# Fourth mixer: the state space part in chunks of 8 steps, with states at the chunk ends alone

## The chip, the cores and the metric

The kernel runs on one core of one Trainium2 chip, in one launch. The metric is the device time of that core in microseconds (us), the median of several runs. Its engines are TensorE (PE, matrix products; PEld its weight loads), VectorE (DVE), ScalarE (ACT), GpSimd (POOL, hardly used here) and SyncE (SP), which issues most of the DMAs. Each engine takes its instructions in the order in which they stand in its queue, so an instruction that waits also holds up all that stands behind it.

## The reference, cut to what matters

The model is a row of four mixer layers, the last two of them with a feed-forward part each, on a sequence of S = 512 rows of width 1024. The change touches the first half of the fourth mixer, the state space model (S5) on 256 channels in 16 groups of 16, with 64 complex states each:

```python
def s5_ssm(u, a_re, a_im, log_dt, b_re, b_im, c_re, c_im, d_skip, w_glu, b_glu):
    ...
    mag = jnp.exp(lr * dt)
    ab_re = mag * jnp.cos(li * dt)
    ab_im = mag * jnp.sin(li * dt)
    ...
    bu_re = jnp.einsum('bsgh,gph->bsgp', ug, bb_re)
    bu_im = jnp.einsum('bsgh,gph->bsgp', ug, bb_im)
    ...
    _, _, x_re, x_im = lax.associative_scan(combine, (aa_re, aa_im, bu_re, bu_im), axis=1)
    y = (jnp.einsum('bsgp,ghp->bsgh', x_re, c_re) - jnp.einsum('bsgp,ghp->bsgh', x_im, c_im)
         + d_skip[None, None] * ug)
    z = jax.nn.gelu(y)
    return z * jax.nn.sigmoid(z @ w_glu + b_glu)

def odd_mixer_2(t, ...):
    proj = t @ w_in
    y_c = s5_ssm(proj[..., :o1], ...)
    y_d = mla_attention(proj[..., o1:o2], proj[..., o2:o3], proj[..., o3:], ...)
    return jnp.concatenate([y_c, y_d], axis=-1) @ w_out
```

`mla_attention` has six heads; its keys and queries are made from two normed low rank pieces (`cn`, `cth` in the kernel). The state recurrence is x[t] = a x[t-1] + B u[t], and the output C x[t] + D u[t].

## The kernel before, in words

The program is a row of phases: two mixers (E1, O1), the third mixer E2 with its feed-forward part F0, the fourth mixer O2 with F1. Weights come by `wload` (line 126 is its DMA on SyncE): a raw piece `wr` (3 buffers), which ScalarE rounds to `wh` (line 133) and VectorE turns into the rest `wl` (line 116); five buffers of each. Every large product is three products of these halves (`mm3`, lines 145, 148, 149). An output projection `outp` keeps four pairs of PSUM banks, "P", "Z", "O" and "W" by their tags, one for each block of 128 rows.

Which instruction of an engine comes first is set by the Tile scheduler from priorities (`prio`), and `hold` ties one instruction behind another. `s5_setup` is called ahead of F0's output projection, so its vector work and its few products lie in F0; its products go to bank "W", which is also that of the fourth row block.

The state space part before: `s5_setup` writes for each of 8 channel blocks a table `rot` of 128 x 1280 (cosines and sines of all 512 steps and the block's input matrix) to DRAM. In O2 `s5(j)` fetches one (640 KB), makes two products of 128 x 512 (`bur`, `bui`), turns them with 12 vector operations of 128 x 512 and two scans, and `s5_out(j)` multiplies the result with C into a bank `py`. The 8 rounds are spread by `s5_step`: one ahead of `projS` (the projection of the low rank pieces), two ahead of the keys `kn` and queries `qn`, one behind each head, the rest behind the sixth. A head `attn` has four row blocks: scores `sc` in bank "Z", their largest `nm` (VectorE), exponentials `e` (ScalarE), reciprocal `rr` (VectorE), scaling (ScalarE, line 1177), transposes `pw` (line 203), copies `wt`; the product `po` of a head comes with the next head's `flush`. At the end come gelu, the gate's product (`pp<-zs`), its sigmoid, and `outp`.

## Time and profile before

| | us |
|---|---|
| three runs | 1712.09, 1715.67, 1715.69 (median 1715.67) |
| the profiled execution | 1711.21 |
| its span, first to last instruction | 1709.4 |
| TensorE busy | 1656.5 (97%) |
| VectorE busy | 950.2 (56%) |
| ScalarE busy | 677.7 (40%) |
| mean granted TensorE clock | 0.987 |

Busy time is a share of the whole span; the change is in two stretches of it, F0's output projection (from about 1001 us) and O2 (from about 1130 to 1340 us), and those are to be read by themselves. TensorE's busy time includes products whose ends are modelled, so it says where the engine had work, not that it ran at its best.

### The profile page before, as it was taken

To read this page: it belongs to the slowest core of one execution; us is meant where nothing else is said; L and a number is where in the kernel's file an instruction comes from. 1 tells how busy PE (TensorE), PEld (TensorE's weight loads), DVE (VectorE), ACT (ScalarE), POOL (GpSimd) and SP (SyncE) were. 2 spreads that over 40 slices of the span, in tenths; PEclk is the share of its full clock that TensorE was granted. 3 is DMA by queue.
4 is the path that set the end of the run, shared out by engine and by line. 5 is a ranking of instruction groups with operands and counts; after the bars stand their busy time and mean duration, and the time that the engine had idled before them with its cause. 6 is when DMAs were issued, how large, how long until landed. Compare 5 with 4: busy or idle time off the path is not lost.

```text
span 1709.4 us, 20684 instructions
## 1 busy us (share of the span) xinstructions
PE 1656.5 (97%) x8072; PEld 1323.6 (77%) x8072; DVE 950.2 (56%) x1801; ACT 677.7 (40%) x1192; POOL 2.0 (0%) x8
## 2 busy tenths in 40 slices
...
GB/s 203 85 38 74 91 181 105 75 25 99 62 205 116 74 87 33 84 187 99 99 99 97 91 151 200 165 123 81 31 31 197 111 100 99 99 95 90 99 160 50
DMA packets 53169, 179.07 MB, mean 105 GB/s; under 512 B 5696, under 2 KB 8256, under 8 KB 52944
## 3 DMA queue, kind: packets, MB, share of 16 engines
...
q14 instruction: 34, 0.28, 0.1%
q0 software_dynamic: 32, 0.07, 0.0%
HBM read 159.63 MB, written 18.10 MB: 104 GB/s over the span
## 4 chain that ended last, share of the span: by engine, by line
PE 85%; DVE 7%; ACT 4%; DMA 2%; issue 1%; ACTq 0%; DVEq 0%; SPq 0%
PE pp L145 17%; PE pp L148 17%; PE pp L149 17%; PE y L145 7%; PE y L149 7%; PE y L148 7%; PE pt L203 2%; PE po L368 2%; PE pl L625 1%; PE pw L203 1%; PE sc L822 1%; PE po L481 1%; DMA wr<-in_e2out 1%; PE pc L764 0%; DMA nw<-in_nw 0%
## 5 line engine op out<-in xcount | busy, mean ns | idle before, releaser
L116 DVE TENSOR_TENSOR wl<-wr,wh 128x1024 fp32r<-128x1024 f32 (+2 forms) x224 | 271.3, 1213 | 343.8 <-ACT wh L133 338.5
L133 ACT CAST wh<-wr 128x1024 fp32r<-128x1024 f32 (+2 forms) x224 | 233.4, 1043 | 523.4 <-PE pp L148 399.2
L148 PE MATMUL pp<-xl,wh 128*128 128x512 f32 (+1 forms) x1184 | 428.5, 362 | 0.0
L145 PE MATMUL pp<-xh,wh 128*128 128x512 f32 (+1 forms) x1184 | 426.0, 361 | 1.2 <-ACT xh L235 1.2
L149 PE MATMUL pp<-xh,wl 128*128 128x512 f32 (+1 forms) x1184 | 425.8, 360 | 0.0
L145 PEld LDWEIGHTS pp<-xh,wh 128*128 128x128 f32 x1184 | 223.8, 190 | 35.6 <-ACT xh L235 2.5
L148 PEld LDWEIGHTS pp<-xl,wh 128*128 128x128 f32 x1184 | 224.7, 190 | 33.8 <-issue 1.9
L149 PEld LDWEIGHTS pp<-xh,wl 128*128 128x128 f32 x1184 | 224.4, 190 | 33.4 <-issue 2.1
L145 PE MATMUL pp<-wh,xh 128*128 128x512 f32 (+1 forms) x320 | 126.4, 395 | 1.4 <-ACT sg L777 1.4
L148 PE MATMUL pp<-wl,xh 128*128 128x512 f32 (+1 forms) x320 | 126.5, 395 | 0.0
L149 PE MATMUL pp<-wh,xl 128*128 128x512 f32 (+1 forms) x320 | 125.4, 392 | 0.0
L145 PE MATMUL y<-wh,ah 128*128 128x512 f32 x288 | 112.7, 391 | 0.2
L148 PE MATMUL y<-wl,ah 128*128 128x512 f32 x288 | 112.3, 390 | 0.0
L149 PE MATMUL y<-wh,al 128*128 128x512 f32 x288 | 112.2, 389 | 0.0
L1238 DVE TENSOR_TENSOR act<-g,pp 128x512 f32<-128x512 f32 x44 | 30.2, 686 | 132.8 <-PE pp L149 131.4
L145 PEld LDWEIGHTS pp<-wh,xh 128*128 128x128 f32 x320 | 60.2, 188 | 13.4 <-ACT sg L777 1.8
L148 PEld LDWEIGHTS pp<-wl,xh 128*128 128x128 f32 x320 | 60.3, 188 | 11.7 <-issue 1.1
L149 PEld LDWEIGHTS pp<-wh,xl 128*128 128x128 f32 x320 | 60.2, 188 | 11.5 <-issue 0.6
L145 PEld LDWEIGHTS y<-wh,ah 128*128 128x128 f32 x288 | 54.1, 188 | 12.4 <-ACT bbz L998 1.1
L322 DVE TENSOR_TENSOR yn<-y,nw 128x512 f32<-128x512 f32 x48 | 31.8, 686 | 56.9 <-ACT yn L320 52.7
L790 DVE SCALAR_TENSOR_TENSOR ycv<-up,vec,ycv 128x512 f32<-128x512 f32 x90 | 63.2, 739 | 0.4
L149 PEld LDWEIGHTS y<-wh,al 128*128 128x128 f32 x288 | 54.1, 188 | 11.1
...
## 6 DMA issues: line engine op xcount, KB each, us to landing
...
```

What stands on the lines that cost most here:

```text
L116: return self.nc.vector.tensor_tensor(l, src, h.bitcast(F32), ALU.subtract)
L133: c = nc.scalar.copy(h, raw)
L145: r = mm(out, lhsT=a[0], rhs=b[0], start=first, stop=False)
L148: mm(out, lhsT=a[0], rhs=b[1], start=False, stop=False)
L149: return mm(out, lhsT=a[1], rhs=b[0], start=False, stop=last)
L203: self.nc.tensor.transpose(out, in_, self.ident)
L322: nc.vector.tensor_tensor(yn[j], yb[b][j], postw[j], ALU.mult)
L368: self.nc.tensor.matmul(po[:, tb * P : tb * P + P], lhsT=wt[:, sb, tb * P : tb * P + P], rhs=v[:, sb, c], start=sb == 0, stop=sb == tb)
L481: nc.tensor.matmul(po[r, sb * P :], lhsT=sv[:, sb, h * 64 : h * 64 + 64], rhs=wt[:, sb, sb * P :], start=sb == 0, stop=sb == 3)
L625: nc.tensor.matmul(pl[:, c4 * 64 : c4 * 64 + 64].rearrange("p (n x) -> p n x", x=H), lhsT=k[:, c4 * P : c4 * P + P], rhs=rh, start=True, s ...
L790: V.scalar_tensor_tensor(y, up[:, j : j + 512], self.v("dw", 4 * j + t), y, ALU.mult, ALU.add)
L1238: nc.vector.tensor_tensor(act[k // 4][:, k % 4], g, ps, ALU.mult)
```

## The change

The state space part now works in 64 chunks of 8 steps. Inside a chunk the output is one product with a triangular kernel (`s5k`), the chunk's input is brought to its end state by one product with a matrix `s5m`, and only the 64 end states are scanned, so that one set of vector operations and two scans over 512 columns (8 blocks x 64 chunks) serves all blocks.

- `s5_setup` makes those matrices: powers of a in small tables, 24 vector operations of 128 x 512 in four groups (`mi`, `mx`, `mg`), 16 transposes (`pbb`) and 32 products (`pk`) into bank "W", a small rotation table of 64 steps, and writes them to DRAM. The eight tables of 512 steps and the 16 products `pbb` are gone.
- `uT` is copied with its steps regrouped, written to DRAM (`s5u`) and read back by 16 DMAs of 16 x 8 x 64 elements (runs of 256 B).
- `s5_in`, behind the first piece of queries: 32 products of 64 x 64 into two banks "Z" (`z`), one set of vector operations, two scans.
- `s5_out`, behind heads 0 and 1: 24 products of 64 (or 63) columns in bank "P", a copy `yo`, 8 DMAs to DRAM (`s5y`, 256 B runs), one read back (`yt`), and on VectorE `yt` plus the skip term. Its matrices come by `s5_maps`, 2 + 8 DMAs.
- gelu may start behind head 4's exponentials, the sigmoid is tied behind the last.

```diff
 (s5_setup, the constants of the chunks)
+        for jj in range(2):
...
+            for ri, (p0, p1, op) in enumerate(((pr, pi, ALU.subtract), (pi, pr, ALU.add))):
+                m = self.U(name="mi")
+                m4 = m.rearrange("p (j s h) -> p j s h", j=4, s=8)
+                tt(m4, rh(bn[:, 0]), rp(p0, 0), ALU.mult)
+                tt(x4, rh(bn[:, 1]), rp(p1, 0), ALU.mult)
+                tt(m, m, x, op)
                 pt = self.bank("W", "pbb")
                 for c in range(4):
-                    self.nc.tensor.matmul(pt[32 * c : 32 * c + 32, 0:P], lhsT=w[2][:, 4 * jj + c], rhs=self.ident, start=True, stop=True)
...
+                    self.tr(pt[:, P * c : P * c + P], m[:, P * c : P * c + P])
+                o = self.U(name="mt")
+                nc.scalar.copy(o, pt)
+                nc.sync.dma_start(self.s5m[:, 1024 * ri + 512 * jj : 1024 * ri + 512 * jj + 512], o)
...
+            pk = self.bank("W", "pk")
+            for c in range(4):
+                for (lo_, hi_, rhs) in ((0, 16, lambda ri: cn[:, ri, 4 * jj + c]),
+                                        (16, 128, lambda ri: go[ri][:, c, 0:7].rearrange("p t h -> p (t h)"))):
+                    for ri in range(2):
+                        nc.tensor.matmul(pk[32 * c : 32 * c + 32, lo_:hi_], lhsT=bb[:, ri, 4 * jj + c], rhs=rhs(ri),
+                                         start=ri == 0, stop=ri == 1)
-        for j in range(8):
-            a, b, m = self.U(name="ra"), self.U(name="rb"), self.U(name="rm")
...
-            sincos(c, a, b, m)
-            nc.sync.dma_start(self.rot[j, :, 0:S], c)
-            nc.sync.dma_start(self.rot[j, :, S : 2 * S], a)
 (odd2)
         def keep(i, ps):
-            nc.scalar.copy(uT[:, i], ps)
+            nc.scalar.copy(uT[:, i].rearrange("p (s c) -> p c s", s=8), ps.rearrange("p (c s) -> p c s", s=8))
+            nc.sync.dma_start(ud[P * i : P * i + P], uT[:, i])
+            for s in range(8):
+                nc.sync.dma_start(ut[i][16 * s : 16 * s + 16].rearrange("p (g c) -> p g c", c=64), dv(ud)[:, s, 8 * i : 8 * i + 8])
+        def s5_in(after):
+            im, rt = self.A4(name="s5im"), self.A4(name="s5rt")
...
+            pz = [self.bank("Z", "z") for _ in range(2)]
...
+            for j in range(8):
+                for ri in range(2):
+                    for g in range(2):
+                        n = 2 * j + g
+                        r = nc.tensor.matmul(pz[ri][64 * g : 64 * g + 64, 64 * j : 64 * j + 64], lhsT=imv[:, ri, j, 64 * g : 64 * g + 64],
+                                             rhs=ut[n // 8][:, (n % 8) * 64 : (n % 8) * 64 + 64], start=True, stop=True)
...
+        def s5_out(jj, x, omv, tv):
+
+            py = self.bank("P", "py")
+            for n in range(8 * jj, 8 * jj + 8):
...
+                nc.tensor.matmul(py[:, o : o + 64], lhsT=tv[:, n % 8], rhs=ut[jj][:, o : o + 64], start=True, stop=False)
+                for ri in range(2):
+                    nc.tensor.matmul(py[:, o + 1 : o + 64], lhsT=omv[:, ri, j % 4], rhs=x[g][ri][:, j, 0:63], start=False, stop=ri == 1)
+            yo = self.U(name="yo")
+            nc.scalar.copy(yo, py)
+            for s in range(8):
+                nc.sync.dma_start(dv(yd)[:, s, 8 * jj : 8 * jj + 8], yo[16 * s : 16 * s + 16].rearrange("p (g c) -> p g c", c=64))
+            y = self.U(name="yt")
+            nc.sync.dma_start(y, yd[P * jj : P * jj + P])
+            V.scalar_tensor_tensor(y, uT[:, jj], self.v("dsk", jj), y, ALU.mult, ALU.add)
...
+                if pc == 0:
+                    xs = s5_in(kept)
...
         for hd in range(6):
             attn(hd)
-            s5_step(1, "P")
+            if hd < 2:
+                s5_out(hd, xs, *maps[hd])
+                maps[1] = s5_maps(1) if hd == 0 else None
...
-        s5_step(8, "P")
...
-            self.hold(r, self.last_e)
+            self.hold(r, gelu_after)
```


**The order, place 1: TensorE, F0's output projection.** `y` are its products (numbers 8143 to 8148 are the banks of the first three row blocks, 8149 and 8150 those of "W"; wh with ah are piece and activation). Before, the setup's products stood ahead of all `y`:

```order
L148 MATMUL pp1335_7803<-xl1084_5998,wh1333_7799 128x512
L149 MATMUL pp1335_7803<-xh1082_5996,wl1334_7800 128x512
L994 MATMUL pbb1341_7962<-cst_77,bb1340_7958 32x128 [waits DVE_49]
L994 MATMUL pbb1341_7962<-cst_77,bb1340_7958 32x128 x3
L994 MATMUL pbb1343_7974<-cst_77,bb1340_7958 32x128 x4
L145 MATMUL y1382_8143<-wh1391_8153,ah1393_8157 128x512 [waits Activation_49]
L148 MATMUL y1382_8143<-wl1392_8154,ah1393_8157 128x512
L149 MATMUL y1382_8143<-wh1391_8153,al1394_8158 128x512
L145 MATMUL y1383_8144<-wh1391_8153,ah1393_8157 128x512
L148 MATMUL y1383_8144<-wl1392_8154,ah1393_8157 128x512
```

Now there are 54 products `y` of the first three row blocks ahead of the first transpose, which waits for VectorE's `mi`:

```order
L149 MATMUL y1382_8148<-wh1394_8219,al1389_8158 128x512
L145 MATMUL y1377_8143<-wh1397_8251,ah1388_8157 128x512
L203 MATMUL pbb1352_8014<-cst_77,mi1351_8010 128x128 [waits DVE_49]
L203 MATMUL pbb1352_8014<-cst_77,mi1351_8010 128x128 x3
L148 MATMUL y1377_8143<-wl1398_8252,ah1388_8157 128x512
L149 MATMUL y1377_8143<-wh1397_8251,al1389_8158 128x512
L145 MATMUL y1378_8144<-wh1397_8251,ah1388_8157 128x512
...
L203 MATMUL pbb1355_8026<-cst_77,mi1354_8022 128x128 [waits DVE_49]
L203 MATMUL pbb1355_8026<-cst_77,mi1354_8022 128x128 x3
L1067 MATMUL pk1359_8044<-s5cn1349_8003,bb1346_7994 32x16 [waits Activation_49]
```

and the first `y` in a bank "W" comes only behind the second group of `pbb` and the first of `pk`, the second behind the last `pk`:

```order
L203 MATMUL pbb1366_8082<-cst_77,mi1365_8078 128x128 x3
L1067 MATMUL pk1370_8100<-s5cn1349_8003,bb1346_7994 32x16 [waits Activation_49]
L1067 MATMUL pk1370_8100<-s5cn1349_8003,bb1346_7994 32x16
L145 MATMUL y1383_8149<-wh1386_8153,ah1388_8157 128x512 [waits Activation_49]
L148 MATMUL y1383_8149<-wl1387_8154,ah1388_8157 128x512
...
L1067 MATMUL pk1370_8100<-mg1369_8095,bb1346_7994 32x112
L149 MATMUL y1383_8149<-wh1400_8283,al1403_8288 128x512
L145 MATMUL y1384_8150<-wh1386_8153,ah1388_8157 128x512 [waits Activation_49]
L148 MATMUL y1384_8150<-wl1387_8154,ah1388_8157 128x512
```

So the setup's products moved from ahead of the projection into it, and five weight pieces' worth of "W" products (8149, 8150) moved behind them.

**Place 2: O2, where the third piece of queries (the rotary part, `pp` of 128 x 384) is made.** Before, on TensorE, a projection, a score block `sc`, and the next projection follow each other:

```order
L145 MATMUL pp1644_9599<-wh1637_9576,cth1529_9146 128x384
L148 MATMUL pp1644_9599<-wl1638_9577,cth1529_9146 128x384
L149 MATMUL pp1644_9599<-wh1637_9576,ctl1530_9147 128x384
L1172 MATMUL sc1680_9722<-kn1608_9471,qn1610_9473 128x384 [waits DVE_49]
L145 MATMUL pp1649_9618<-wh1637_9576,cth1529_9146 128x384 [waits DVE_49,PE_49]
L148 MATMUL pp1649_9618<-wl1638_9577,cth1529_9146 128x384
L149 MATMUL pp1649_9618<-wh1637_9576,ctl1530_9147 128x384
L145 MATMUL pp1649_9618<-wh1637_9576,cth1529_9146 128x384
L148 MATMUL pp1649_9618<-wl1638_9577,cth1529_9146 128x384
L203 MATMUL pt1643_9594<-cst_77,r1640_9587 128x128 [waits DVE_49]
```

Now the last products `z` stand ahead of two score blocks, which wait for VectorE to leave the banks "Z", and of a projection that waits for the bank of the one before it:

```order
L1151 MATMUL z1605_9493<-uT1514_9032,s5im1602_9486 64x64 x2
L1151 MATMUL z1604_9492<-uT1514_9032,s5im1602_9486 64x64 x2
L1151 MATMUL z1605_9493<-uT1514_9032,s5im1602_9486 64x64 x2
L1274 MATMUL sc1662_9740<-kn1580_9413,qn1582_9415 128x384 [waits DVE_49,PE_49]
L1274 MATMUL sc1667_9756<-kn1580_9413,qn1582_9415 128x512 [waits DVE_49,PE_49]
L145 MATMUL pp1630_9625<-wh1618_9583,cth1523_9165 128x384 [waits DVE_49]
L148 MATMUL pp1630_9625<-wl1619_9584,cth1523_9165 128x384
L149 MATMUL pp1630_9625<-wh1618_9583,ctl1524_9166 128x384
L145 MATMUL pp1630_9625<-wh1618_9583,cth1523_9165 128x384
L148 MATMUL pp1630_9625<-wl1619_9584,cth1523_9165 128x384
L203 MATMUL pt1624_9601<-cst_77,r1621_9594 128x128 [waits DVE_49]
L203 MATMUL pt1624_9601<-cst_77,r1621_9594 128x128 x2
```

On VectorE the rows that free those banks stand within the vector operations of `s5_in` (`t11622_9595` and `t21623_9596` read the bank `pp1620_9587`):

```order
L1165 TENSOR_TENSOR sa1609_9533<-z1604_9492,s5rt1603_9487 128x512 [waits DMAHW3_49,PE_49]
L1166 TENSOR_TENSOR sb1610_9534<-z1605_9493,s5rt1603_9487 128x512 [waits DMAHW4_49,PE_49]
L1167 TENSOR_TENSOR sa1609_9533<-sa1609_9533,sb1610_9534 128x512 [waits DVE_49]
L1168 SCALAR_TENSOR_TENSOR yr1607_9531<-s5rt1603_9487,sa1609_9533 128x512 [waits DMAHW5_49,DVE_49]
L1166 TENSOR_TENSOR sb1610_9534<-z1604_9492,s5rt1603_9487 128x512
L1165 TENSOR_TENSOR sa1609_9533<-z1605_9493,s5rt1603_9487 128x512 [waits DVE_49]
L1167 TENSOR_TENSOR sa1609_9533<-sa1609_9533,sb1610_9534 128x512 [waits DVE_49]
L1168 SCALAR_TENSOR_TENSOR yi1608_9532<-s5rt1603_9487,sa1609_9533 128x512 [waits DVE_49]
L433 TENSOR_TENSOR t11622_9595<-pp1620_9587,cst_77 128x384
L1169 TENSOR_TENSOR sa1609_9533<-yr1607_9531,s5rt1603_9487 128x512 [waits DVE_49]
L1170 TENSOR_TENSOR sb1610_9534<-yi1608_9532,s5rt1603_9487 128x512
L434 TENSOR_TENSOR t21623_9596<-pp1620_9587,cst_77 128x6x32
```

So vector work that was spread over eight rounds now stands in one run, with the rotary operations between its rows.

**Place 3: behind head 0's output part.** Before, on VectorE, a row of the state space round stood between the heads' `nm` and `rr`, with a wait for VectorE alone:

```order
L1082 TENSOR_TENSOR yi1699_9776<-yi1699_9776,tab1695_9769 128x512
L1176 RECIPROCAL rr1713_9827<-nm1711_9823 128x1 [waits Activation_49]
L418 TENSOR_REDUCE nm1716_9839<-sc1715_9835 128x1
L1083 TENSOR_TENSOR yi1699_9776<-yr1698_9775,yi1699_9776 128x512 [waits DVE_49]
L416 MEMSET sc1720_9852 64x64 [waits PE_49]
L416 MEMSET sc1733_9894 64x64 [waits PE_49]
L1176 RECIPROCAL rr1718_9843<-nm1716_9839 128x1 [waits Activation_49]
L418 TENSOR_REDUCE nm1721_9856<-sc1720_9852 128x1 [waits DVE_49]
```

Now `yt` stands between them and waits for a DMA, and the next `nm` is behind it:

```order
L418 TENSOR_REDUCE nm1690_9864<-sc1689_9860 128x1 [waits DVE_49]
L416 MEMSET sc1699_9893 64x64 [waits PE_49]
L1278 RECIPROCAL rr1692_9868<-nm1690_9864 128x1 [waits Activation_49]
L1208 SCALAR_TENSOR_TENSOR yt1679_9822<-uT1514_9032,vec_79,yt1679_9822 128x512 [waits DMAHW2_49]
L418 TENSOR_REDUCE nm1695_9880<-sc1694_9876 128x1 [waits DVE_49]
L416 MEMSET sc1708_9946 64x64 [waits PE_49]
L1278 RECIPROCAL rr1697_9884<-nm1695_9880 128x1 [waits Activation_49]
L418 TENSOR_REDUCE nm1700_9897<-sc1699_9893 128x1 [waits DVE_49]
```

On SyncE the DMA that it waits for is behind the eight writes (the last five shown) and two reads of the next half's kernels:

```order
L1205 DMA s5y_9034<-yo1678_9812 16x8x64 [waits DMAHW3_49]
L1205 DMA s5y_9034<-yo1678_9812 16x8x64 [waits DMAHW4_49]
L1205 DMA s5y_9034<-yo1678_9812 16x8x64 [waits DMAHW5_49]
L1205 DMA s5y_9034<-yo1678_9812 16x8x64 [waits DMAHW6_49]
L1205 DMA s5y_9034<-yo1678_9812 16x8x64 [waits DMAHW7_49]
L1188 DMA s5mt1680_9825<-s5k_8008 16x8x128 [waits DMAHW0_49]
L1188 DMA s5mt1680_9825<-s5k_8008 16x8x128 [waits DMAHW1_49]
L1207 DMA yt1679_9822<-s5y_9034 128x512 [waits DMAHW5_49,DMAHW4_49,DMAHW6_49,DMAHW3_49,DMAHW7_49,DMAHW2_49,DVE_49]
L1188 DMA s5mt1680_9825<-s5k_8008 16x8x128 x2
```

So the largest of the next score block can be taken only when the trip to DRAM and back has ended.

## Rows read from the trace of the kernel before

**Rows 1.** Windows view: busy us of each engine by stretch (instructions), granted clock, DMA.

```profile
core 0: us, PE busy (x) PEld busy (x) DVE busy (x) ACT busy (x) POOL busy (x), PEclk, DMA share, GB/s
1000.00:1050.00 50.00, 49.76 (x243) 39.81 (x242) 46.51 (x78) 22.02 (x39) 0.00 (x0) 1.00 0.52 174
1165.00:1188.00 23.00, 22.22 (x80) 12.68 (x79) 21.44 (x41) 12.03 (x27) 0.00 (x0) 1.00 0.41 130
1188.00:1210.00 22.00, 21.00 (x97) 14.45 (x96) 13.35 (x36) 11.85 (x28) 0.00 (x0) 1.00 0.15 51
1210.00:1250.00 40.00, 33.28 (x112) 16.73 (x110) 33.69 (x69) 17.28 (x44) 0.00 (x0) 0.91 0.06 18
```

**Rows 2.** Waits of TensorE, 1125 to 1345: us in total, times, longest us.

```profile
PE pw L203 <- ACT e L1177: 7.4, 6, 3.1
PE sc L1172 <- ACT e L420: 4.1, 4, 1.0
```

**Rows 3.** Timeline of TensorE, 1163 to 1174: start us, us, instruction, count, idle before.

```profile
1165.88 1.02 PE L1070 MATMUL bur<-uT,tab 128*128 128x512 f32 x2
...
1167.97 1.04 PE L1093 MATMUL py<-sa,s5c 128*32 128x512 f32 x2
1168.95 0.44 PE L203 MATMUL pt<-cst,cn 128*128 128x128 f32 x2
...
1172.16 0.74 PE L145 MATMUL pp<-cth,wh 128*128 128x512 f32 x2 [0.57 <-ACT cth L1058]
```

**Rows 4.** Timeline of TensorE, the heads: first, a middle and the last one.

```profile
1206.43 0.44 PE L203 MATMUL pw<-cst,e 128*128 128x128 f32 x2
...
1211.39 1.02 PE L1070 MATMUL bur<-uT,tab 128*128 128x512 f32 x2
1212.25 1.02 PE L1070 MATMUL bui<-uT,tab 128*128 128x512 f32 x2
1213.11 2.32 PE L1187 MATMUL po<-wt,va 128*128 128x512 f32 x8
...
1277.57 0.44 PE L203 MATMUL pw<-cst,e 128*128 128x128 f32 x2 [0.65 <-ACT e L1177]
...
1292.79 0.78 PE L145 MATMUL pp<-zs,wh 128*128 128x512 f32 x1
```

**Rows 5.** Groups by form, VectorE, 1165 to 1292: busy us, mean ns, idle before.

```profile
L1077 DVE TENSOR_TENSOR_SCAN yi<-s5sm,sa 128x512 f32<-128x512 f32 x7 | 8.6, 1224 | 0.2
...
L1080 DVE TENSOR_TENSOR sa<-sa,sb 128x512 f32<-128x512 f32 x7 | 4.8, 682 | 0.0
...
L433 DVE TENSOR_TENSOR t<-pp,cst 128x384 f32<-128x384 f32 x4 | 2.2, 551 | 1.0 <-PE pp L149 1.0
```

**Rows 6.** Groups by form, ScalarE, 1205 to 1290.

```profile
L1177 ACT ACTIVATE e<-e,rr 128x384 f32<-128x384 f32 x6 | 3.7, 616 | 7.5 <-DVE rr L1176 7.5
...
L1208 ACT ACT_TABLE_LOAD x1 | 1.3, 1283 | 0.0
```

**Rows 7.** Timeline of TensorE, 1000 to 1009: the first setup products and F0 down.

```profile
1000.87 0.64 PE L994 MATMUL pbb<-cst,bb 128*32 128x128 f32 x16
1001.44 0.50 PE L145 MATMUL y<-wh,ah 128*128 128x512 f32 x1
```

**Rows 8.** Timeline of VectorE, 985 to 1003: where the setup chain begins.

```profile
996.78 1.22 DVE L116 TENSOR_TENSOR wl<-wr,wh 128x1024 fp32r<-128x1024 f32 x1
```

**Rows 9.** Timeline of TensorE, 313.9 to 316, another stage: 64 column products.

```profile
314.13 1.00 PE L625 MATMUL pl<-q,k 128*128 128x64 f32 x8
314.94 0.47 PE L145 MATMUL pp<-xh,wh 128*128 128x512 f32 x1
```

**Rows 10.** DMA issues: KB each, median us from issue to landing.

```profile
rot<-ra SPq DMA_DIRECT2D x8, 256.0 KB, 2.1
rot<-rc SPq DMA_DIRECT2D x8, 256.0 KB, 2.6
```

**Rows 11.** The setup table tile: duration ns min/median/max of a DMA issue on SyncE.

```profile
L1013 SPq DMA_DIRECT2D rot<-rc x8: 319/320/382, 1015.9 to 1064.2; - x8
```

More of the change, by code (lines that the diff above doesn't have):

```diff
@@ new lines, in s5_setup @@
+        v3 = lambda n, name: self.U(8 * n, name=name).rearrange("p (j n) -> p j n", j=8)
+        pr, pi, mag = v3(16, "pwr"), v3(16, "pwi"), v3(16, "mag")
+        turns(pr, pi, dp, 16)
+        V.memset(mag[:, :, 7:8], 1.0)
+        rho3 = rho.unsqueeze(2)
+        V.tensor_copy(mag[:, :, 8:9], rho3)
+        for d in range(2, 9):
+            tt(mag[:, :, 7 + d : 8 + d], mag[:, :, 6 + d : 7 + d], rho3, ALU.mult)
+        for d in range(1, 8):
+            V.tensor_copy(mag[:, :, 7 - d : 8 - d], mag[:, :, 7 + d : 8 + d])
@@ L987, in s5_setup @@
+        w = self.U(256, name="bw").rearrange("p (j h) -> p j h", j=8)
         for ri in range(2):
-            V.tensor_tensor(w[0], bc[:, ri], b8(fre), ALU.mult)
-            V.tensor_tensor(w[1], bc[:, 1 - ri], b8(fim), ALU.mult)
-            V.tensor_tensor(w[2], w[0], w[1], ALU.subtract if ri == 0 else ALU.add)
-            for jj in range(2):
+            tt(bb[:, ri], bc[:, ri], b8(fre), ALU.mult)
+            tt(w, bc[:, 1 - ri], b8(fim), ALU.mult)
+            tt(bb[:, ri], bb[:, ri], w, ALU.subtract if ri == 0 else ALU.add)
```

165 lines of the change are left out of this document (106 added, 59 removed).

## The prediction

> **What bounds the kernel now.** The page gives TensorE 97% of the span, so I read the two stretches that the change touches, each by itself. The windows view [rows 1] shows F0's output projection full: 49.76 us of 50 have work on TensorE. O2 is full at its start too (22.22 of 23, 21.00 of 22), but not in the heads: 33.28 of 40 us, at a granted clock of 0.91, with VectorE at 33.69. The waits [rows 2] say for what: the transposes `pw` wait 7.4 us for ScalarE's scaled exponentials, the scores 4.1 us for a bank. ScalarE in turn [rows 6] stands idle 7.5 us ahead of one form of the scaling alone, until VectorE has the reciprocal: in the heads VectorE's queue, full of state space rows, is late, and TensorE with it. The timelines [rows 3, 4] give the lengths of O2's pieces: 1165.88 the end of `projS`; 1172.16 the first key product; 1206.43 the first transpose `pw` of head 0; 1277.57 that of head 5; 1292.79 the gate.
>
> **Prices of single products.** A product of 128 x 512 in f32 is two instructions and holds the queue 0.86 us (`bur`, 1211.39 to 1212.25 [rows 4]); one of `py` 0.98 (1167.97 to 1168.95 [rows 3]). With 64 columns and full weights an instruction costs 0.81 / 8 = 0.10 [rows 9]; with 32 columns of weights side by side in the four column groups 0.57 / 16 = 0.036 [rows 7]. The new narrow products lie between these two rows.
>
> **F0.** Removed: 16 `pbb`, two bursts of 0.57 [rows 7], -1.1. Added: 16 transposes of 128 x 128, about 0.09 each between the two prices, +1.5; 32 `pk`, 64 instructions, 2.3 to 6.4 by the two prices, and I take 4.0, since half of them have 16 columns. They stand inside the projection, which has no idle time to hide them [rows 1]. Then the waits. In place 1 of the order, 55 `y` stand ahead of the first transpose: if they start at about 1000.9 in place of 1001.44 [rows 7], at this stretch's pace of (50 - 1.1) / (243 - 32) = 0.23 a product [rows 1] TensorE is there at 1013.6. VectorE starts the run that ends with the first `mi` at 996.78 [rows 8]. Ahead of it stand 2 splits at 1.2, 9 rows of 128 x 512 that were there before at 0.6, 3 new ones at 0.68 [rows 5], and 38 narrow ones, which no row prices; at 0.25, a third of the wide one, they take 9.5. That gives 19.5 us, 1016.3, a wait of 2.5 in round numbers (0 to 5). From there VectorE has 23 more rows at 0.68 = 15.6 to the last `mg`, TensorE 49 `y`, 11.3, and the narrow products between, together about 15: +1.0 of wait. The "W" banks must be copied out twice before the fourth row block may start: +0.6, no row of its own (0 to 2). Sum: 1.5 + 4.0 + 2.5 + 1.0 + 0.6 - 1.1 = **+8.5**, from +1 to +14. The eight tables of 512 steps go from VectorE's 46.51 us of work there [rows 1] at no gain: TensorE was full over them, and is the bound. If VectorE's late rows then held up the weight splits behind them, the loss would be more.
>
> **O2, piece by piece.** (a) Ahead of `projS`' end one round's two products go: 2 x 0.86 = **-1.7**.
>
> (b) From `projS` to the first key product it is 6.3 us, and 4.6 of these held state space products [rows 3]. They were a filling: the product waits for `cth`. The last `cn` transposes stood behind two `py`, though, and can now come earlier. The gain is between 0 and 1.9; I take **-1.7**, since VectorE and ScalarE lose rows ahead of it too.
>
> (c) From there to head 0's first `pw`: 34.3 us now. Away: one `bui` and four `py`, -4.8. In: 32 `z`, 64 instructions, 2.3 to 6.4; 3.8 taken. Then place 2: behind `z` TensorE has two score blocks (1.6 us), and a projection whose bank is freed by VectorE's fifteenth row of the new run: ten of 0.65, two scans of 1.2, three of 0.5 [rows 5], 10.5 us. Nothing else stands ahead in its queue, so it waits 10.5 - 1.6 = 8.9, and 2.0 more for the next bank. The 1.8 us that it stood idle in these windows [rows 1] are in this wait. -4.8 + 3.8 + 10.9 - 1.8 = **+8.1** (+2 if `z` lies at the lower price and half the run is hidden, +13).
>
> (d) Head 0 to head 5: 71.1 us now [rows 4]. TensorE's share of it is 33.28 / 40 = 0.83, 11.8 a head; without ten `bur`/`bui` and eight `py`, 16.4 us, a head's own work is 8.5. The time less those products is 10.9 a head. I take 8.9, near the work, since the idle time behind VectorE's queue [rows 2, 6] goes: 44.5 for five. In come two `s5_out` of 24 products, 48 instructions each: 1.7 each by the lower price, 4.9 by the upper, and I take the upper, whose row has the same full weights and 64 columns. And two waits (place 3): the copy 0.6, eight writes at 0.32 [rows 11], a landing of 2.3, the read's landing of 2.3 (2.1 and 2.6 for 256 KB [rows 10]), 0.75 for `yt`: 8.4 us until VectorE can take the next `nm`. TensorE has some 4 us of scores and transposes ahead of it, so it waits 4.4 each, 9 together. 44.5 + 9.8 + 9.0 = 63.3: **-7.8** (-16 to +8).
>
> (e) Head 5's end: gelu now stands among its exponentials, so two more table loads of 1.28 [rows 6] on ScalarE, less the last round's `py`: **+1.5** (-1 to +3).
>
> Seven of the eight rounds' vector work (12 x 0.68 + 2 x 1.2 = 10.6 us each [rows 5]) and 5 MB of table loads fall out at no further gain than (d): VectorE bounds TensorE only through the heads.
>
> **A rule that speaks against the change.** The trips to DRAM are in 256 B runs, and the trace has no DMA of that kind to price; I took those of the contiguous 256 KB [rows 10]. The Trainium skill ("DMA: Bandwidth & Descriptors", Specifications) wants at least 512 B a transfer for line rate, and says that below it the engine reads, modifies and writes. No run here shows that yet; rival 3 below is what it would do.
>
> **Sum.** +8.5 - 1.7 - 1.7 + 8.1 - 7.8 + 1.5 = +6.9 us. The profiled execution took 1711.2, so its successor takes 1718.1: 0.40% more. The median of the three runs shown stands 4.5 above the profiled one, the lowest 0.9; I don't add a part of that, since three runs don't tell which is the rule. TensorE's own work falls by 11.4 us (16 x 0.86 + 16 x 0.98 + 1.1 = 30.5 away, 5.5 + 3.8 + 9.8 in); it is the waits that take this back. About 0.2%, 3.4 us, is what a measurement of this kernel can tell from no change.
>
> **The rivals.** 1: *Work, not waits, sets the time.* If the new waits only take the place of old ones (7.4 and 4.1 us [rows 2]), the kernel gets faster. It ends on the other side of my forecast. For it: in the heads VectorE's rows are what TensorE waits for, and they go. Against: in places 1 to 3 the order puts a wait on VectorE or on a DMA at the head of TensorE's queue. Its price: without the 10.9 of (c) and the 9.0 of (d) it is 1718.1 - 19.9 = 1698, with half of them left 1708. It decides once less than 10 of these 19.9 us show up as idle time.
>
> 2: *The narrow products lie at the lower price.* 48 + 48 instructions of `s5_out` at 0.036 in place of 0.10 save 6.3, `z` 1.5, `pk` 1.7: -9.5, so 1708.6, and 1712 where the saved time is partly spent at the same waits. For it: the products of [rows 7] run so. Against: `s5_out` uses all columns of the weights, as the 0.10 row does.
>
> 3: *The 256 B runs land late.* Each of the four landings in (d) counts in full, as do the sixteen reads of `uT` ahead of `z`. At 5 us in place of 2.3, (d) grows by 4 x 2.7 = 10.8: 1729. For it: no row of such a DMA; against: each of the writes moves 32 KB, an eighth of the 256 KB that land in 2.1 to 2.6 us [rows 10].
>
> **How the numbers follow.** My sum, 1714 to 1723: 0.41, of which 0.07 lies within 0.2%. Rival 1: 0.28, all faster. Rival 2: 0.18, of it 0.05 faster and 0.13 within 0.2%. Rival 3: 0.13, slower. Slower: 0.34 + 0.13 = 0.47; within 0.2%: 0.20; faster 0.33. The time is that of the sum, 1718. The range reaches down into rival 1 and up to rival 3: 1700 to 1728 leaves out about 0.2; the sum's own is 1714 to 1723.
>
> **What would show each step.** F0: waits of `pbb` and `pk` for `mi` and `mg` of about 3.5 us. (c): TensorE idle 9 to 11 us behind `z`, released by VectorE's t rows. (d): first `pw` of head to head about 9 us for heads 2 to 5; waits of TensorE that end with `nm` behind `yt`, 4.4 each; `s5_out` 4.9 long. (e): three gelu or exp table loads near head 5. It is wrong if heads take 8 us or less and `yt` waits less than 2 us each, or if a trip to DRAM takes over 4 us.

## The result and the profile after

| | us |
|---|---|
| before, median | 1713.88 |
| after, median of 4 runs | 1730.13 (1725.62 to 1733.64) |
| ratio, 95% interval | 1.0086 [1.0066, 1.0107] |
| after, the profiled execution | 1730.91, its span 1729.1 |

The change makes the kernel slower by 0.86%. The prediction had the sign and less than half of the size: its sum was 6.9 us over the profiled execution of before, and the profiled executions are 19.7 apart; its range ended at 1728. The page of the changed kernel (span, busy time by engine, granted clock in 40 slices):

```profile
span 1729.1 us, 20904 instructions
...
PE 1656.7 (96%) x8216; PEld 1341.5 (78%) x8216; DVE 877.1 (51%) x1710; ACT 671.3 (39%) x1174; POOL 1.6 (0%) x8
...
PEclk9999999999999998899999999998798999999999
```

VectorE lost 73 us of work, as the change means it to. TensorE's busy time stayed where it was (1656.5 before), though 16 `bur`/`bui` and 16 `py` are gone; a dip in the clock is new, in slices 28 to 31 (43.2 us each), where O2 lies. TensorE's idle time is the span less its busy time: 52.9 us before, 72.4 now, 19.5 more. By the stages that the prediction used (their ends from TensorE's timelines):

| stage | before | after | difference | predicted |
|---|---|---|---|---|
| F0's output projection, first `y` to the last transposes ahead of O2 | 132.15 | 138.19 | +6.0 | +8.5 |
| (a) to the last product of `projS` | 32.08 | 31.73 | -0.4 | -1.7 |
| (b) to the first key product | 6.49 | 5.70 | -0.8 | -1.7 |
| (c) to head 0's first `pw` | 34.27 | 46.13 | +11.9 | +8.1 |
| (d) to head 5's first `pw` | 71.14 | 73.22 | +2.1 | -7.8 |
| (e) to the gate `pp<-zs` | 15.22 | 12.19 | -3.0 | +1.5 with the next |
| to the transposes of F1's third row block | 50.86 | 55.01 | +4.1 | |

The windows view of the changed kernel, over F0, (a), (c), then (d) with (e), and the last stage:

```profile
1000.98:1139.17 138.19, 135.11 (x681) 110.52 (x680) 82.81 (x147) 47.72 (x78) 0.00 (x0) 1.00 0.43 148
1139.17:1170.90 31.73, 31.32 (x164) 27.91 (x164) 12.42 (x36) 12.75 (x33) 0.00 (x0) 0.89 0.25 69
1176.60:1222.73 46.13, 36.47 (x188) 26.20 (x189) 24.11 (x48) 15.78 (x32) 0.00 (x0) 0.84 0.38 115
1222.73:1308.14 85.41, 66.28 (x296) 45.24 (x294) 18.14 (x71) 46.08 (x113) 0.00 (x0) 0.84 0.07 16
1308.14:1363.15 55.01, 53.93 (x249) 43.91 (x250) 34.38 (x50) 30.77 (x54) 0.00 (x0) 0.97 0.51 179
```

The last product of the sixth head (`po`) stood ahead of the gate before and stands behind it now, so the last two rows of the table are to be read together: +1.1. The stages (c) and (d) of the kernel before, and (d) of the changed one, by the same view:

```profile
1172.16:1206.43 34.27, 33.32 (x141) 22.74 (x141) 27.68 (x52) 16.39 (x33) 0.00 (x0) 1.00 0.17 57
1206.43:1277.57 71.14, 60.67 (x207) 30.76 (x207) 60.10 (x129) 34.81 (x90) 0.00 (x0) 0.95 0.10 35
...
1222.73:1295.95 73.22, 59.33 (x274) 40.88 (x273) 16.14 (x63) 34.18 (x92) 0.00 (x0) 0.86 0.09 19
```

In (c) TensorE is idle 46.13 - 36.47 = 9.7 us, and in the heads 19.1, at a granted clock of 0.84 in both; before, (c) stood at 1.00 and the heads at 0.93. VectorE, in the heads 33.69 of 40 us busy before [rows 1], now has 18.14 in 85: it is no longer short of time, and TensorE waits all the same. The waits of TensorE, 1130 to 1370, say for what:

```profile
PE sc L1274 <- ACT e L420: 9.8, 6, 5.9
PE pw L203 <- ACT e L1279: 6.5, 6, 3.1
PE pp L145 <- DVE t L435: 4.0, 2, 2.8
PE sc L1274 <- DVE sb L1166: 3.9, 1, 3.9
...
PE z L1151 <- DMA uT<-s5u: 1.3, 1, 1.3
```

The first two rows answer to [rows 2], with the longest single wait at 5.9 in place of 1.0 for `sc` (the names of the wait are ScalarE's, the cause is behind them, below); the next two are new. TensorE's timeline shows where they lie (start, us, instruction, in brackets the idle time before it and its releaser):

```profile
1193.44 0.34 PE L148 MATMUL pp<-wl,cth 128*128 128x384 f32 x1
1193.62 0.35 PE L149 MATMUL pp<-wh,ctl 128*128 128x384 f32 x1
...
1197.24 1.15 PE L1151 MATMUL z<-uT,s5im 128*64 128x64 f32 x32 [1.27 <-DMA uT<-s5u]
1202.31 3.27 PE L1274 MATMUL sc<-kn,qn 128*128 128x384 f32 x4 [3.92 <-DVE sb L1166]
1208.40 0.44 PE L145 MATMUL pp<-wh,cth 128*128 128x384 f32 x1 [2.82 <-DVE t L435]
...
1212.47 0.69 PE L145 MATMUL pp<-wh,cth 128*128 128x384 f32 x1 [1.17 <-DVE t L435]
1212.95 0.52 PE L148 MATMUL pp<-wl,cth 128*128 128x384 f32 x1
1213.27 0.52 PE L149 MATMUL pp<-wh,ctl 128*128 128x384 f32 x1
...
1237.51 0.49 PE L1274 MATMUL sc<-kn,qn 128*128 128x128 f32 x2 [1.14 <-ACT e L420]
...
1248.11 1.65 PE L1274 MATMUL sc<-kn,qn 128*128 128x384 f32 x2 [5.93 <-ACT e L420]
...
1268.28 0.90 PE L203 MATMUL pw<-cst,e 128*128 128x128 f32 x3 [3.13 <-ACT e L1279]
```

This is place 2 of the order: two score blocks behind `z` wait until VectorE has left the banks, then two projections wait for its rotary rows. And a second thing: the 384 column products follow each other every 0.18 us ahead of these waits (1193.44 to 1193.62) and every 0.32 behind them (1212.95 to 1213.27). The windows view has the granted clock for it. 0.50 is the lower of the clock's two levels, 1.2 GHz, and 1.00 the upper, 2.4 GHz. First the kernel before, the first 4 us of the keys; then the changed one, there, behind the waits of place 2, and around the wait of 5.93 us (1242.18 to 1248.11):

```profile
1172.16:1176.16 4.00, 3.79 (x15) 2.46 (x15) 3.93 (x6) 2.49 (x6) 0.00 (x0) 1.00 0.05 12
...
1176.60:1180.60 4.00, 4.00 (x9) 2.87 (x10) 0.54 (x1) 1.69 (x4) 0.00 (x0) 0.50 0.38 122
1210.60:1214.80 4.20, 3.03 (x11) 2.53 (x10) 3.89 (x10) 0.50 (x2) 0.00 (x0) 0.50 0.66 185
1241.20:1252.90 11.70, 5.77 (x18) 3.73 (x18) 2.41 (x8) 3.11 (x9) 0.00 (x0) 0.50 0.20 48
```

So the same work takes longer in these stretches: the keys get through 9 instructions in 4 us in place of 15, and the pair of score instructions that takes 1.65 us at 1248.11 (head 1) takes 0.91 in head 3, where TensorE waits little:

```profile
1280.48 0.91 PE L1274 MATMUL sc<-kn,qn 128*128 128x384 f32 x2
```

Ahead of each of the three TensorE had idled: 4.3 of the 5.7 us of (b), where the state space products stood before; 3.92, 2.82 and 1.17 us at place 2; 5.93 us at place 3. At place 3, VectorE's timeline:

```profile
1245.89 0.75 DVE L1208 SCALAR_TENSOR_TENSOR yt<-uT,vec,yt 128x512 f32<-128x512 f32 x1 [6.27 <-DMA yt<-s5y]
1246.56 0.68 DVE L418 TENSOR_REDUCE nm<-sc 128x1 f32<-128x512 f32 x1
...
1266.75 0.75 DVE L1208 SCALAR_TENSOR_TENSOR yt<-uT,vec,yt 128x512 f32<-128x512 f32 x1 [3.42 <-DMA yt<-s5y]
```

VectorE stands 6.27 us at `yt`, the next `nm` starts behind it at 1246.56, and ScalarE's timeline has the exponentials released by that `nm`, TensorE's score by those (1248.11 above). It also has the copy `yo` 8.06 us late, behind 5.5 us of `py`, with exponentials right behind it in the queue, and gelu's table loads in head 5:

```profile
1236.41 0.59 ACT L1203 COPY yo<-py 128x512 f32<-128x512 f32 x1 [8.06 <-PE py L1201]
1236.89 0.48 ACT L420 ACTIVATE e<-sc,nm 128x256 f32<-128x256 f32 x1
...
1247.28 0.69 ACT L420 ACTIVATE e<-sc,nm 128x512 f32<-128x512 f32 x1 [7.01 <-DVE nm L418]
...
1298.12 1.28 ACT L1314 ACT_TABLE_LOAD   x1
1299.41 1.06 ACT L1314 ACTIVATE yg<-yt 128x512 f32<-128x512 f32 x1
...
1300.99 1.28 ACT L420 ACT_TABLE_LOAD   x1
```

The trip itself, by the DMA issues (KB each, median us to landing):

```profile
yt<-s5y SPq DMA_DIRECT2D x2, 256.0 KB, 3.8
...
uT<-s5u SPq DMA_DIRECT2D x16, 32.0 KB, 2.1
s5y<-yo SPq DMA_DIRECT2D x16, 32.0 KB, 1.8
```

### The profile page after: what moved, and what is told of

Read it like the earlier page. It is cut to its first block, busy times and chain, and to the rows that moved or that the text cites. A ratio compares the mean times of both kernels' runs of the same rounds, so it can differ in the third digit from the quotient of the medians.

```text
span 1729.1 us, 20904 instructions
## 1 busy us (share of the span) xinstructions
PE 1656.7 (96%) x8216; PEld 1341.5 (78%) x8216; DVE 877.1 (51%) x1710; ACT 671.3 (39%) x1174; POOL 1.6 (0%) x8
## 3 DMA queue, kind: packets, MB, share of 16 engines
q8 instruction: 65, 1.06, 0.3%
## 4 chain that ended last, share of the span: by engine, by line
PE 84%; DVE 7%; ACT 4%; DMA 3%; issue 1%; SPq 0%; ACTq 0%; DVEq 0%
PE pp L145 17%; PE pp L148 17%; PE pp L149 17%; PE y L149 7%; PE y L145 7%; PE y L148 7%; PE pt L203 2%; PE po L368 2%; PE pl L625 1%; PE pw L203 1%; PE sc L822 1%; DVE wl L116 1%; PE po L1289 1%; PE sc L1274 1%; PE sc L1275 1%
## 5 line engine op out<-in xcount | busy, mean ns | idle before, releaser
L145 PEld LDWEIGHTS pp<-wh,xh 128*128 128x128 f32 x320 | 60.2, 188 | 13.2 <-ACT sg L777 1.8
L149 PEld LDWEIGHTS pp<-wh,xl 128*128 128x128 f32 x320 | 60.2, 188 | 11.5 <-issue 0.6
L148 PEld LDWEIGHTS pp<-wl,xh 128*128 128x128 f32 x320 | 60.3, 188 | 11.4 <-issue 0.9
L148 PEld LDWEIGHTS y<-wl,ah 128*128 128x128 f32 x288 | 54.1, 188 | 11.2 <-issue 0.2
```

Source lines behind the costliest of these rows:

```text
L145: r = mm(out, lhsT=a[0], rhs=b[0], start=first, stop=False)
L148: mm(out, lhsT=a[0], rhs=b[1], start=False, stop=False)
L149: return mm(out, lhsT=a[1], rhs=b[0], start=False, stop=last)
```

## The experiments

Three explanations were set against each other: the new waits at places 2 and 3 cost the time; or the granted clock, which fell, costs it, whatever the waits; or ScalarE's order (the copy `yo`, gelu among the exponentials) does. Each kernel is the changed one with the edit shown; its time is the median of 5 to 12 runs, and its ratio is that to the kernel before on the same chip. Its trace is that of one run.

**The skip term later** (place 3 alone): `yt`'s row on VectorE is emitted behind head 3 and held behind its last reciprocal.

```diff
-            V.scalar_tensor_tensor(y, uT[:, jj], self.v("dsk", jj), y, ALU.mult, ALU.add)
+            skip.append((y, jj))
...
+            if hd == 3:
+                for y, jj in skip:
+                    r = V.scalar_tensor_tensor(y, uT[:, jj], self.v("dsk", jj), y, ALU.mult, ALU.add)
+                    self.hold(r, self.last_r)
```

> The two vector rows that add the skip term to yt are tied behind head 3's last reciprocal; nothing else is changed. Theory A (the trip to DRAM holds up VectorE's queue, and the idle time also costs TensorE its granted clock): TensorE's waits of 5.9 and 3.1 us in heads 1 to 2 go, and the granted clock of that stretch rises from 0.82 to 0.9 or more; 1730 becomes 1715 to 1721. Rival B (waits alone, the clock is not touched): 9 us less, 1721. Rival C (ScalarE's copy yo between the exponentials is what holds the heads up, the trip is hidden): 1727 to 1730.

1722.58, ratio 1.0053 [1.0035, 1.007]: by the ratios 6 to 10 us less than the changed kernel (1.0086 and, below, 1.0109), and not the 1727 of rival C. Its waits in the heads:

```profile
PE sc L1274 <- ACT e L420: 3.7, 5, 1.4
PE pw L203 <- ACT e L1279: 3.4, 5, 1.9
PE py L1199 <- DMA s5mt<-s5k: 2.7, 1, 2.7
```

The 5.9 is gone, and the heads' stage is shorter by 5.6 us (79.82), all of it idle time (19.1 to 13.0); the clock there is 0.87, not the 0.9 of theory A. Part came back: the second `py` now arrives before its matrices have landed, and behind that wait its products take 9.6 us in place of 6.1.

**The scan behind the rotary rows** (place 2 alone): ScalarE copies the two `z` banks, so they come free at once, and VectorE's run is emitted behind the rotary loop.

```diff
+            for p in pz:
+                c = self.U(name="zc")
+                nc.scalar.copy(c, p)
...
+        def s5_scan(rot, pz):
...
                 nc.scalar.activation(qrT[:, 0:3, sl], pt[:, :384].rearrange("p (k t) -> p k t", k=3), AF.Copy, scale=MLA_SC)
+            xs = s5_scan(*zin)
```

> The two banks z are copied out by ScalarE at once, and the vector run of the state space part is written behind the rotary rows of the queries. Theory A (VectorE's run holds the banks that TensorE needs next): the waits of 3.9, 2.8 and 1.2 us behind z go, the granted clock of 1176 to 1223 rises from 0.84; 1730 becomes 1717 to 1722. Rival C (the run only moves: head 0's first rows then wait behind it): 1727 to 1731, with the wait at head 0's scores.

1723.37, 1.0060 [1.0041, 1.0079]: 4 to 8 less by the ratios. The window of (c):

```profile
1180.97:1219.03 38.06, 33.07 (x194) 24.84 (x195) 19.09 (x39) 17.74 (x34) 0.00 (x0) 0.95 0.47 138
```

(c) falls from 46.13 to 38.06, the heads stay at 85.44. Of these 8.1 us, 4.7 are idle time (9.66 to 4.99) and 3.4 busy time (36.47 to 33.07), the clock being back at 0.95.

**Gelu behind the last exponentials**, as before the change:

```diff
-            self.hold(r, gelu_after)
+            self.hold(r, self.last_e)
```

> gelu is tied behind the last exponential again, as in the kernel before; two table loads and two gelu of 1.08 us leave head 5's chain. Theory A (they stand on the path of the last head): -2 to -4 us, 1726 to 1728. Rival C (the gate's product then starts later by as much as the head ends earlier): 1729 to 1732.

1729.98, 1.0093 [1.0074, 1.0112]: nothing by itself that the time shows.

**The idle time filled**: 16 products of 128 x 512 into a bank that nobody reads, four each behind `projS`, behind `z` and behind a score block of heads 2 and 3.

```diff
+        def fill(after, n):
+            d = self.bank("O", "fill")
+            for i in range(n):
+                with self.prio(1200):
+                    r = nc.tensor.matmul(d, lhsT=self.ident, rhs=uT[:, 0], start=True, stop=True)
+                self.hold(r, after)
```

> Sixteen products of 128 x 512 into a bank that nobody reads are put into four places where TensorE waits (four each: behind the last transpose of projS, behind z, and behind a score block of heads 2 and 3); they are work on top, 13.8 us at the full clock, and leave nothing out. Theory A (idle time drops the granted clock, and the drop costs some 11 us of the 19.7): the granted clock of 1171 to 1293 rises from 0.84 to 0.9 or more and the time falls, to 1720 to 1727, in spite of the added work. Rival B (waits alone): the added work is longer than the waits in part, so 1730 to 1740.

1731.51, 1.0114 [1.0095, 1.0133]: no gain. In (c) the clock is up to 0.92 and TensorE's idle time down to 6.8, and the stage is 43.54 long; the windows of (b), of the first 4 us of the keys, and of (c):

```profile
1168.96:1178.53 9.57, 5.87 (x16) 2.63 (x15) 4.53 (x12) 3.71 (x13) 0.00 (x0) 0.82 0.58 177
1178.53:1182.53 4.00, 4.00 (x16) 2.46 (x15) 0.00 (x0) 2.12 (x4) 0.00 (x0) 1.00 0.00 0
1178.53:1222.07 43.54, 36.75 (x198) 25.36 (x197) 23.57 (x47) 15.16 (x30) 0.00 (x0) 0.92 0.36 110
```

(b) is longer by 3.9 and takes back more than (c) gains. The reason is where the filling stands. In (b) it is behind the last transposes, so its products run behind most of the idle time (4.3 us of it in the changed kernel, 3.7 here) and ahead of the keys; the keys then run at 1.00, 16 instructions in 4 us for 9. Behind `z` it does lie in a wait:

```profile
1201.36 1.74 PE L1284 MATMUL sc<-kn,qn 128*128 128x384 f32 x4 [0.30 <-DVE sb L1176]
1207.45 0.44 PE L145 MATMUL pp<-wh,cth 128*128 128x384 f32 x1 [4.35 <-DVE t L435]
```

The score blocks take 1.74 us in place of 3.27, but the next wait is 4.35 in place of 2.82, since VectorE sets its end. So the same products get faster where the idle time ahead of them is filled, and the time is not gained: the filling is in the way itself, or another engine ends the wait.

**The changed kernel once more** (c0), since the next kernels ran on another chip, then **both waits gone** (e5, the first two edits together):

> The changed kernel itself once more, so that the others of this group are compared with it on the same chip. Both theories: 1726 to 1733, granted clock of O2's stages between 0.79 and 0.89, differing from run to run.

> Both edits together: yt behind head 3, and the vector run behind the rotary rows. Theory A (the two waits are in different places and add up, and with less idle time the granted clock of the heads stays higher): 1712 to 1717. Rival C (the next wait takes over: the kernels s5mt of the second half, for which TensorE waited 2.7 us when yt went): 1718 to 1722, with that wait in the trace.

1731.77, 1.0109 [1.0088, 1.013], and 1714.50, 1.0012 [0.9997, 1.0028]. The two edits add: 17.3 us, and the kernel is where it was before the change.

**The setup at the program's start**: `s5_setup` is called ahead of the first mixer in place of ahead of F0's output projection.

```diff
-    if "O2" in ph and "F0" not in ph:
-        n.s5_setup()
+    n.s5_setup()
```

> The setup of the matrices is called at the start of the program in place of ahead of F0's output projection; O2 is unchanged. Theory A (in F0 it stands in a full TensorE and costs the 6.0 us by which that stretch is longer; at the start TensorE waits for data anyway): 1722 to 1726. Rival D (its vector rows hold up the first mixer by as much): 1729 to 1740.

1742.19, 1.0170 [1.0147, 1.0192]. F0's first `y` starts at 1020.19 in place of 1000.98, and only 8.8 of those 19.2 us come back by the end of `projS`. F0's stage itself is 130.45 long (138.19 in the changed kernel, 132.15 before), so its 6.0 us are the setup's. In the first 100 us VectorE has 79.06 us of work (64.15 in the changed kernel), and TensorE 88.02 (91.74), so the start is no free place:

```profile
0.00:100.00 100.00, 88.02 (x507) 69.44 (x507) 79.06 (x275) 50.94 (x86) 1.53 (x8) 0.89 0.47 162
```

**The state space input ahead of the keys**: the skip edit, and `s5_in` right behind `projS`, its DMAs ahead of others.

```diff
         with self.prio(300):
+            xs = s5_in(None)
             kn = [self.A4(name="kn") for _ in range(2)]
...
-                if pc == 0:
-                    xs = s5_in(kept)
```

> yt behind head 3 as in the first run, and s5_in is written right behind projS, ahead of the keys, with its loads ahead of the weights of the output projection. VectorE has only 4.2 us of work in the 16 us of keys and queries, so the run of 11 us would lie there. Theory A: head 0's first transpose comes 8 to 11 us earlier after projS, 1711 to 1716. Rival E (the 1 MB of matrices land later than projS ends, and z then holds up the keys in TensorE's queue): 1720 to 1728, with a wait of z for s5im of 4 us or more.

1717.96, 1.0019 [1.0004, 1.0035]: 3.5 us more than both waits gone (1714.50), on the same chip, and between the two expectations. `z` does not wait for its matrices, but the waits of place 2 are still 6.8 of 7.9 us (2.6 for `sb`, 4.2 for `t`): half of the products `z` still come behind the first queries, and VectorE's run behind them, with the rotary rows in it.

**Both waits gone, and gelu last** (e6):

> The two edits of e5 and gelu behind the last exponential. Alone that third edit gave nothing that shows in the time, though its trace had the stretch from the gate to the end of the projection 2 us shorter. Theory A (two table loads and two long gelu leave the last head's chain, and now nothing else covers them): 1710 to 1713. Rival C (the gate starts later by as much): 1714 to 1716.

1709.50, 0.9962 [0.9947, 0.9977]: faster than before. The window of the heads:

```profile
1214.85:1288.27 73.42, 62.98 (x298) 42.37 (x297) 24.62 (x83) 46.44 (x112) 0.00 (x0) 0.94 0.10 21
```

The heads are 12.0 shorter than in the changed kernel. Against both waits gone alone it is 5.0 us by the medians, 8.6 by the ratios (on two chips). How much of this is gelu's place is open. The two traces are 11.4 us apart, and 5.4 of these lie ahead of head 5, where gelu does not stand: the waits there are nearly the same (6.4 and 5.9 us idle), but in head 1 the clock of the one trace falls to 0.50, and that of the other stays at 1.00. From head 5's first `pw` to the transposes of F1's third row block the trace is 6.6 us shorter (70.53 to 63.90); where gelu's place was the only edit it was 2.9 (67.20 to 64.34), and the time showed nothing of it.

**`z` ahead of the keys as well**: the last kernel with `s5_in` called right behind `projS`, as above; its copies `zc` come with it, the scan stays behind the rotary rows.

> e6 with z written ahead of the keys, its loads ahead of the weights of the output projection, so that z may lie in the 5.6 us in which TensorE waits for the first key product. Theory A: 2 to 4 us less than e6, and higher granted clock in the keys. Rival E (z waits for its 1 MB and holds up the keys): the same or up to 3 us more.

1706.82, 0.9942 [0.9926, 0.9959]: the best here, 0.58% under the kernel before and 1.4 to 1.7% under the change as it was made. (c) is down to 35.99, with 3.8 us idle; half of `z` now lies in (b), which is 0.3 longer. The first 4 us of the keys stay at 0.50, so the higher clock that was expected there did not come.

**The copy `yo` on VectorE**, on each of the last two kernels:

```diff
-            nc.scalar.copy(yo, py)
+            V.tensor_copy(yo, py)
```

> e6 with the copy yo of the chunk outputs on VectorE in place of ScalarE, where it stands ahead of the next head's exponentials and waits for 24 products. Theory A (ScalarE can then work on the next head while TensorE makes these products): 3 to 6 us less than e6. Rival C (on VectorE it holds up the next head's largest-of-row in the same way): within 1 us of e6.

> Both of these on e6. Theory A: their gains add up, 1705 to 1709, which would be faster than the kernel before by 0.3% or more. Rival: what remains of F0's 6.0 us and of the two output parts in the heads keeps it at 1711 to 1715.

1713.28, 0.9986 [0.9974, 0.9997], and 1709.53, 0.9954 [0.993, 0.9977]: no gain. The first is 3.8 us slower than without the edit, which neither expectation had; the second, 2.7, is within its interval. The heads' stage is 73.55 long in the first, as without the edit (73.42), so ScalarE's `yo` ahead of the exponentials is not what holds the heads; the trace has most of the loss in (a) and (c), at a lower clock, where nothing was edited, and its cause is open. In the second the heads are 79.55 long at 0.86, with the waits of its parent (10.8 us idle, 9.9 there) and 5.1 us more busy time.

The two stages side by side (length, TensorE busy and idle in us, granted clock; (c), then the heads to the gate):

| kernel | (c) | busy | idle | clock | heads | busy | idle | clock |
|---|---|---|---|---|---|---|---|---|
| before | 34.27 | 33.32 | 1.0 | 1.00 | 86.36 | 72.92 | 13.4 | 0.93 |
| after | 46.13 | 36.47 | 9.7 | 0.84 | 85.41 | 66.28 | 19.1 | 0.84 |
| after, again | 46.67 | 37.15 | 9.5 | 0.78 | 83.66 | 64.22 | 19.4 | 0.88 |
| skip later | 46.98 | 37.09 | 9.9 | 0.79 | 79.82 | 66.81 | 13.0 | 0.87 |
| scan behind | 38.06 | 33.07 | 5.0 | 0.95 | 85.44 | 65.88 | 19.6 | 0.84 |
| gelu last | 43.95 | 34.71 | 9.2 | 0.85 | 86.28 | 69.57 | 16.7 | 0.86 |
| idle filled | 43.54 | 36.75 | 6.8 | 0.92 | 86.69 | 74.44 | 12.3 | 0.86 |
| skip, scan | 37.73 | 32.91 | 4.8 | 0.95 | 78.20 | 66.60 | 11.6 | 0.85 |
| skip, scan, gelu | 38.21 | 33.17 | 5.0 | 0.95 | 73.42 | 62.98 | 10.4 | 0.94 |
| and `z` early | 35.99 | 32.22 | 3.8 | 0.91 | 73.55 | 63.70 | 9.9 | 0.93 |
| skip, `s5_in` early | 41.84 | 34.37 | 7.5 | 0.84 | 80.29 | 67.78 | 12.5 | 0.85 |
| skip, scan, gelu, `yo` | 40.94 | 34.78 | 6.2 | 0.90 | 73.55 | 62.71 | 10.8 | 0.95 |
| the same, `z` early | 34.68 | 31.12 | 3.6 | 0.94 | 79.55 | 68.77 | 10.8 | 0.86 |

In (c) four kernels have the same instructions (after, again, skip later, gelu last). Their idle time is 9.2 to 9.9; their busy time goes from 34.71 to 37.15 while the clock goes from 0.85 to 0.78. So between these four the clock makes some 2 us; against the kernel before, whose (c) ran at 1.00, it makes more: by the prediction's prices the work there should have fallen by 1.0, and busy time rose by 3.2.

The single runs say the same of the whole kernel. The twelve of the skip term later, one program, go from 1712.68 us at a mean granted clock of 0.984 to 1729.12 at 0.973. Within the kernels here 0.001 of mean clock goes with about 1.1 us (a line through all their runs, each kernel about its own mean). The change takes the median of the runs' mean clock from 0.984 to 0.9755, so an estimate from these is 9 to 10 us by the clock. Why one run of a program stands higher than the next was not tried.

## Why the prediction was wrong in size

**The step that failed.** "TensorE's own work falls by 11.4 us [...]; it is the waits that take this back." The waits were nearly right: the sum held 6.9 + 11.4 = 18.3 us more idle time, and it is 19.5. The work was not: TensorE's busy time rose by 0.2 us. The prediction priced every product as at the upper clock and put what the clock costs behind the new waits at nothing, though [rows 1] had the heads at 0.91. Nearly all of the missing 11.6 us lies in three stages of O2 whose clock fell (that of (b) fell too, but little work is left there). Busy time by stage, against the work by the prediction's own prices:

| stage | work, predicted | busy time, measured | more than predicted | clock before, after |
|---|---|---|---|---|
| (a) | -1.7 | +0.1 | 1.8 | 0.95, 0.89 |
| (b) | -4.6 | -4.5 | 0.1 | 1.00, 0.83 |
| (c) | -1.0 | +3.2 | 4.2 | 1.00, 0.84 |
| (d) | -6.6 | -1.3 | 5.3 | 0.95, 0.86 |
| (e) and the last | -2.0 | -2.0 | 0.0 | 0.95, 0.92 |

**F0 (+8.5, measured +6.0): right in kind.** Groups of the new products by form there (busy us, mean ns, idle before):

```profile
L1067 PE MATMUL pk<-mg,bb 128*32 128x112 f32 x32 | 2.8, 263 | 0.0
L203 PE MATMUL pbb<-cst,mi 128*128 128x128 f32 x16 | 2.5, 276 | 0.5 <-DVE mi L933 0.5
L1067 PE MATMUL pk<-s5cn,bb 128*32 128x16 f32 x32 | 1.8, 188 | 0.0
```

Busy time grew by 5.2, where I had 4.4. The waits were 0.5 for `mi` and 0.5 for `mt`, in place of 4.1 in all: the narrow vector rows in that chain were priced too high.

**(a), (b): -1.1 in place of -3.4.** In (a) the two products are gone, but the stage ran at 0.89 where it had 0.95; in the second trace of the same kernel it is 30.33 us long at 0.94, -1.75, as predicted. In (b) 1.44 us of work are left in 5.70: TensorE waits 2.24 us for VectorE's `cn`, 1.46 for its `kr` and 0.57 for `cth`. The prediction called the products there a filling; what it missed is that the keys behind the emptied stage then start at 0.50.

**(c), +8.1, measured +11.9: the wait was right, its company was not.** I had TensorE idle 9.1 more; it is 8.7 more. That near is in part luck: place 2 gave 7.9 us (3.92, 2.82, 1.17) where I had 10.9 in another order, and 1.3 for `z` itself came in, which waits for `uT`. Busy time should have fallen by 1.0 (-4.8 + 3.8) and rose by 3.2. `z` was not at fault, with 2.3 us for its 64 instructions. It is the same products at half the pace: some 2 us of it at the first keys (ten instructions in 4.6 us; 2.5 in the filled kernel), the rest behind place 2, the 384 column products at 0.32 in place of 0.18.

**(d), -7.8, measured +2.1: the largest miss.** My 63.3 us were 52.3 of work (five heads at 8.5, and 9.8) and 11.0 idle (0.4 a head, and 9.0 at `yt`). Measured are 59.33 and 13.89, so 7.0 of the 9.9 us are busy time and 2.9 idle.

The idle time behind VectorE's queue went in part: in heads 3 and 4, which have no state space part, it fell from 3.4 to 2.3 us, where I had left 0.8, and their `po` come near my figure (at 1274.95, 1284.15 and 1293.79: 9.2 and 9.6 apart for 8.9). The waits at `yt` are 5.93 + 3.13 = 9.1, as priced, and that is luck, since the trip took longer and the second wait was the shorter for it: from the start of `yo`, 1236.41, to the next `nm`, 1246.56, are 10.2 us, where I had 8.4. Eight writes are issued in 3.65 (0.46 each, priced 0.32), and the read of 256 KB lands in 3.8, priced 2.3. I had priced it by the only 256 KB rows that I showed, which are writes (2.1 to 2.6 [rows 10]); the trace of before also has a read of that size, `s5b<-in_s5bc`, in 3.6. Not priced at all were 2.4 us of other waits in heads 1 and 2, 1.14 of them right behind `yo`.

Of the busy time, `s5_out` is 5.5 and 6.1 long, 11.5 in place of 9.8, and three products of the output projection moved in, 0.7. The rest, over 4 us, is the same products at the lower clock, above all in the 11.7 us around the wait of 5.93, which stand at 0.50.

**(e), +1.5 with the last stage, measured +1.1.** The table loads are there; moving them gave nothing alone (gelu last: 1729.98) and at most 5 to 9 us once the waits were gone, part of it the clock ahead of them.

**The rivals.** *Work, not waits* falls for the change as made: its own bound was that less than 10 of the 19.9 us show as waits, and places 2 and 3 show 7.9 and 9.1. The kernel with the three edits, 1709.50, and the one with `z` early come near its prices (1708 and 1698), by other means: there the new waits were taken out. *The narrow products at the lower price* holds for `z` (0.036 an instruction) and falls for `s5_out` (5.5 / 48 = 0.11), which carried most of it. *The 256 B runs land late* came nearest to the time, 1729, by a mechanism that did not occur: those DMAs land in 1.8 to 2.1 us (medians; 2.9 at most). The 5 us that it put in their place stood on no row, so the near hit is luck. The Trainium skill ("DMA: Bandwidth & Descriptors", Specifications) asks for at least 512 B for line rate; at 32 KB a DMA no lateness shows here, and what it would do at larger sizes no run here shows.

**What it comes to.** Removing the waits at places 2 and 3 and gelu's place gives 1731 - 1709.5, some 21 us. That the sum had as much for these terms (10.9 + 9.0 + 1.5 = 21.4) is luck: between the two traces 13.2 us are idle time and 10.5 busy time (1656.7 to 1646.2). So the waits are shown to be the cause, since the time goes when they go, and the busy time goes with them: at 1646.2 it is 10.3 below the kernel before, near the 11.4 that the prediction had. That the busy time hangs on the clock is shown by the rows at 0.50 and 1.00 and by the filled kernel, whose same products ran faster. What stays open is what part of the time an edit of the clock alone would give back, since the filling added work too, and why two runs with the same waits can differ in the clock, as in the heads of the last kernel.
